# Scores of two chunked recurrences: one native float32 product, or three passes of split operands

## The chip, the cores and the metric

The kernel runs on one core of a Trainium2 chip. The metric is device time in microseconds (us) of one execution. A run executes the whole block once, from the inputs in device memory to the output in device memory.

## The reference, cut to what matters

The block has one layer over 1024 positions of width 1024. It normalises `x`, multiplies by one wide input matrix, and feeds three branches: an mLSTM (matrix memory with gates), a differential attention and a retention. Their outputs are merged, projected, and followed by a gated feed-forward layer. The mLSTM and the retention are recurrences over chunks, with 4 heads of width 256 each. What the change touches is the score product in both of them:

```
# mLSTM, per chunk
s = einsum('blhd,bshd->bhls', qj, kj) * w_intra
num = einsum('bhls,bshe->blhe', s, vj) + einsum('blhd,bhde->blhe', qj, C) * w_int_t
C_new = w_old * C + einsum('bhs,bshd,bshe->bhde', w_k, kj, vj)
# retention, per chunk
s = einsum('blhd,bshd->bhls', qj, kj) * dmask
o = einsum('bhls,bshe->blhe', s, vj) + einsum('blhd,bhde->blhe', qj, R) * xi
R_new = chunk_decay * R + einsum('hs,bshd,bshe->bhde', zeta, kj, vj)
```

All inputs and outputs are float32.

## The kernel before

**Split operands.** Nearly all products are made of three passes. A float32 operand is split by `split_sbuf` (L104 to L106) into a high part, which ScalarE casts to the type float32r (L105), and a low part, the rest, which VectorE subtracts (L106). `mm3` (L108 to L113) then sums three matmuls into one bank of PSUM: high by high (L111), high by low (L112), low by high (L113). The first two have the same stationary operand. A native float32 matmul, without a split, is used in a few places; the scores of the recurrences are one (L690).

**The recurrences.** Both are run in chunks of 128 positions, 8 chunks in each of 4 heads, so 32 chunks each and 64 in all. `pipelined` (L777) goes through the chunks. For each it loads the next chunk's tile `ch` from device memory (`chunk_of`, L639; 128 partitions, eight blocks of 128 columns: two of queries, two of keys, two of a gate, two of values), and then calls three parts. `start` makes the scores (`scores_t`, L687), turns keys and values round by transposes on TensorE (`natural_k`, `natural_v`, L645 to L668), multiplies the scores by the mask (L733 in the mLSTM, L946 in the retention) and splits what the next part multiplies (L739, L950). `end` of the chunk before turns its result round and stores it (L693 to L701). `middle` multiplies scores by values and queries by the carried state into one bank (`chunk_products`, L676), and updates the state (L764, L968) and splits it (`split_state`, L703).

**The queries for the state.** In the mLSTM the queries are scaled per position (L735) and stand in one tile `w` beside the masked scores, 384 columns in all, which are split together. In the retention they are not scaled, but they are copied beside the scores all the same (L948), and split with them (L950). The first chunk of a head has no state and splits 128 columns only.

**The order of work.** Between the three parts of a chunk, `weave` (L1470) takes steps of dense work, 2.6 per unit of weight that `pipelined` yields: two units a chunk. A dense step is here one of seven products of a block of the input projection (`follow`, L373), 12 passes of 512 columns each, with its evacuation and the split of a later weight. A scheduler then writes out the order of each engine's queue from priorities (the order of the program) and from its own estimate of what will be ready; an instruction that it holds to be late is passed by ready ones. On the chip each queue runs in the order written.

**Buffers.** Tiles of up to 512 float32 columns come from one group of 14 buffers (`half_tile`, L96). Score tiles in PSUM come from a group of four banks, those of the dense work from another group of four.

Of the kernel before, what the change touches and what calls it, by code (L numbers as in the profile page):

```python
# [9 lines left out]
F32R = mybir.dt.float32r  # L10
# [5 lines left out]
P = 128  # L16
# [24 lines left out]
def trunk(ctx: ExitStack, tc: tile.TileContext, x, norm_gains, w_in, mlstm_conv, mlstm_gate_bias,  # L41
          diff_lambda, diff_subln, w_mlstm_out, w_diff_out, w_ret_out, w_out, w_ffn_in, w_ffn_out,
          c_ident, c_dist, c_tri, c_ret, c_retcol, c_reset, out):
    nc = tc.nc
# [21 lines left out]
    def psum(dense=False):  # L66

        return psp.tile([P, HALF], F32, tag="d" if dense else "m", bufs=N_D if dense else 8 - N_D, name=nm("ps"))
# [27 lines left out]
    def half_tile(shape=(P, HALF), dtype=F32):  # L96
        return pool.tile(list(shape), dtype, tag="s2k", bufs=N_H, name=nm("s2k"))
# [6 lines left out]
    def split_sbuf(hi, lo, src):  # L104
        nc.scalar.copy(hi, src)  # L105
        nc.vector.tensor_sub(lo, src, hi.bitcast(F32))  # L106

    def mm3(ps, lhs, rhs, start, stop, more=False):  # L108

        (lh, ll), (rh, rl) = lhs, rhs  # L110
        nc.tensor.matmul(ps, lh, rh, start=start, stop=False, skip_group_check=more)  # L111
        nc.tensor.matmul(ps, lh, rl, start=False, stop=False, skip_group_check=more)  # L112
        nc.tensor.matmul(ps, ll, rh, start=False, stop=stop, skip_group_check=more)  # L113
# [556 lines left out]
    def both(t):  # L670
        return t[:, 0], t[:, 1]

    def cols_at(t, a, b):
        return t[0][:, a:b], t[1][:, a:b]

    def chunk_products(u, d, n):  # L676

        num = psum()
        v = both(u["v"])
        mm3(num[:, :n], cols_at(u["w"], 0, P), v, True, u["c"] == 0)  # L680
        if u["c"] > 0:
            for j in range(2):
                st = tuple(t[:, j, :] for t in d["parts"])
                mm3(num[:, :n], cols_at(u["w"], P + j * P, 2 * P + j * P), st, False, j == 1)
        return num

    def scores_t(ch):  # L687
        ps = psum()
        for j in range(2):
            nc.tensor.matmul(ps[:, :P], ch[:, 2 + j, :], ch[:, j, :], start=j == 0, stop=j == 1)  # L690
        return ps[:, :P]

    def finish_chunk(u, spill):  # L693

# [15 lines left out]
    def mlstm_core():  # L710
        def start(u):
            hd, c = u["hd"], u["c"]
            d = ml[hd]
            ch = u["ch"]
            if c == 0:
                wt = d["wt"] = big([P, NT, P], name="wt")
                nc.sync.dma_start(wt, rows_dram[0, hd:hd + 1, :].rearrange("o (c l) -> o c l", l=P).broadcast_to([P, NT, P]))
                wib = d["wib"] = big([P, S], name="wib")
                nc.sync.dma_start(wib, rows_dram[1, hd:hd + 1, :].broadcast_to([P, S]))

                wk = d["wk"] = small([P, NT], "wk")
                nc.vector.tensor_tensor(wk, wt[:, :, P - 1], u_col[:, :, hd], op=ALU.add)
                nc.scalar.activation(wk, wk, AF.Exp)
                nc.vector.tensor_tensor(wt, wt, tri.unsqueeze(1).broadcast_to([P, NT, P]), op=ALU.add)
                for i in range(NT):
                    nc.scalar.activation(wt[:, i, :], wt[:, i, :], AF.Exp, bias=u_col[:, i, hd:hd + 1])
            s_ps = scores_t(ch)
            if c < NT - 1:
                u["kw"] = natural_k(ch, d["wk"][:, c:c + 1])
            u["v"] = natural_v(ch, True)  # L730
            n = 3 * P if c > 0 else P
            w = half_tile([P, n])
            nc.vector.scalar_tensor_tensor(w[:, :P], s_ps, HD ** -0.5, d["wt"][:, c, :], op0=ALU.mult, op1=ALU.mult)  # L733
            if c > 0:
                nc.vector.scalar_tensor_tensor(w[:, P:].rearrange("p (j l) -> p j l", j=2), ch[:, 0:2, :], HD ** -0.5,  # L735
                                               d["wib"][:, c * P:(c + 1) * P].unsqueeze(1).broadcast_to([P, 2, P]),
                                               op0=ALU.mult, op1=ALU.mult)
            u["w"] = half_tile([P, n], F32R), half_tile([P, n], F32R)
            split_sbuf(*u["w"], w)  # L739

        def middle(u):
            hd, c = u["hd"], u["c"]
            d = ml[hd]
            num = chunk_products(u, d, VA)


            ss = square_sum(num[:, :HD], HD, "m")
            den = small([P, 1], "den", bufs=4)
            nc.vector.tensor_scalar(den, num[:, HD:HD + 1], -1.0, em_col[:, c, hd:hd + 1], op0=ALU.mult, op1=ALU.max)
            nc.vector.tensor_tensor(den, num[:, HD:HD + 1], den, op=ALU.max)  # L750
            nc.gpsimd.tensor_scalar(den, den, den, EPS, op0=ALU.mult, op1=ALU.mult)
            fac = small([P, 1], "fac", bufs=4)
            factor(fac, ss, 1.0 / HD, den)
            if c < NT - 1:
                if c == 0:
                    d["st"] = small([P, 2, VA], "st", bufs=1)
                for j in range(2):
                    kv = psum()
                    mm3(kv[:, :VA], cols_at(both(u["kw"]), j * P, (j + 1) * P), both(u["v"]), True, True)
                    st = d["st"][:, j, :]  # L760
                    if c == 0:
                        nc.vector.tensor_copy(st, kv[:, :VA])
                    else:
                        nc.vector.scalar_tensor_tensor(st, st, d["wib"][:, c * P + P - 1:c * P + P], kv[:, :VA],  # L764
                                                       op0=ALU.mult, op1=ALU.add)
                split_state(d)
            u["hn"] = small([P, HD], "hk", bufs=2)
            nc.scalar.activation(u["hn"], num[:, :HD], AF.Copy, scale=fac)

        def end(u):  # L770
            finish_chunk(u, b_dram[0])
            if u["c"] == NT - 1:
                ml[u["hd"]].clear()

        yield from pipelined(m_dram, 0, start, middle, end)
# [152 lines left out]
    def ret_core():  # L928
        retm = half_tile([P, MH, P])
        nc.scalar.dma_start(retm, c_ret)  # L930

        over = small([P, MH], "over", bufs=1)
        nc.vector.reciprocal(over, retc[:, 2 * MH:3 * MH])
        nc.vector.tensor_scalar(over, over, EPS / HD, None, op0=ALU.mult)

        def start(u):
            hd, c = u["hd"], u["c"]
            d = rt[hd]
            ch = u["ch"]
            s_ps = scores_t(ch)  # L940
            if c < NT - 1:
                u["kw"] = natural_k(ch, retc[:, hd:hd + 1])
            u["v"] = natural_v(ch, False)
            n = 3 * P if c > 0 else P
            w = half_tile([P, n])
            nc.vector.tensor_mul(w[:, :P], s_ps, retm[:, hd, :])  # L946
            if c > 0:
                nc.vector.tensor_copy(w[:, P:].rearrange("p (j l) -> p j l", j=2), ch[:, 0:2, :])  # L948
            u["w"] = half_tile([P, n], F32R), half_tile([P, n], F32R)
            split_sbuf(*u["w"], w)  # L950

        def middle(u):
            hd, c = u["hd"], u["c"]
            d = rt[hd]
            num = chunk_products(u, d, HD)
            ss = square_sum(num[:, :HD], HD, "r")
            fac = small([P, 1], "rfac", bufs=4)
            factor(fac, ss, 1.0 / HD, over[:, hd:hd + 1])
            if c < NT - 1:
                kv = psum()  # L960
                for j in range(2):
                    mm3(kv[:, j * HD:(j + 1) * HD], cols_at(both(u["kw"]), j * P, (j + 1) * P), both(u["v"]), True, True)
                kv = kv.rearrange("p (j e) -> p j e", j=2)
                if c == 0:
                    d["st"] = small([P, 2, HD], "st", bufs=1)
                    nc.vector.tensor_copy(d["st"], kv)
                else:
                    nc.vector.scalar_tensor_tensor(d["st"], d["st"], (1.0 - 2.0 ** (-5.0 - hd)) ** P, kv, op0=ALU.mult, op1=ALU.add)  # L968
                split_state(d)
            u["hn"] = small([P, HD], "hk", bufs=2)  # L970
            nc.scalar.activation(u["hn"], num[:, :HD], AF.Copy, scale=fac)

        def end(u):
            finish_chunk(u, b_dram[2])
            if u["c"] == NT - 1:
                rt[u["hd"]].clear()

        yield from pipelined(r_dram, 4 * MH, start, middle, end)


# [387 lines left out]
    for b in BRANCHES:  # L1368
        for o in range(0, KT, 2):
            c = C_G + b * D + o * P  # L1370
# [76 lines left out]
    ps = psum()  # L1447
# [92 lines left out]
```

## Time and profile before

| what | value |
|---|---|
| median of 3 runs | 2629.19 us (2627.92 to 2631.38) |
| the profiled execution, its own time | 2628.78 us |
| its span, first to last instruction | 2627.0 us |
| TensorE (PE) busy | 2520.3 us, 96% |
| VectorE (DVE) busy | 1650.2 us, 63% |
| ScalarE (ACT) busy | 1245.9 us, 47% |
| GpSimd (POOL) busy | 331.8 us, 13% |

PE is the multiplying array, PEld the loading of its stationary operand, which has a record of its own for each matmul. A matmul's record lasts longer than the step to the next one, since matmuls are pipelined: what a matmul costs a full array is the time from its start to the next start. In the timelines, `L690` and the like are lines of the kernel; `s2k` are the tiles of `half_tile`; `x4` says that four like instructions were merged into one row. A native float32 matmul shows two PE records.

### The profile page before, as it was taken

Reading aid. Unit: us, or ns where it says so; the run is one execution under the profiler, and the core shown is the slowest. Engines: PE = TensorE matmul, PEld = TensorE weight load, DVE = VectorE, ACT = ScalarE, POOL = GpSimd, SP = SyncE. Lnnn points to the kernel's source line nnn. Section 1 sums busy time; section 2 is a strip of 40 time slices with the busy share of each in tenths; the row PEclk is TensorE's granted clock in tenths of the full one; section 3 lists DMA queues with packets and bytes.
Section 4 is the critical chain, followed back from the end, with each engine's and each line's share of the span. In section 5 each row is a group of like instructions: output and inputs, shape, how many; then the busy total and the mean of one; then the engine's idle time right before and its main releaser. Section 6 shows DMA issues by size and latency. Waiting matters only on the chain.

```text
span 2627.0 us, 35171 instructions
## 1 busy us (share of the span) xinstructions
PE 2520.3 (96%) x12061; PEld 2058.6 (78%) x12061; DVE 1650.2 (63%) x3164; ACT 1245.9 (47%) x2562; POOL 331.8 (13%) x657
## 2 busy tenths in 40 slices
PE   6989999999999999999999988999989999999997
PEld 5868887888888888888878776778877888888885
DVE  7767777666656666555556665653468655656756
ACT  6554554444444444444446555542365333334444
POOL 0001111000000000000003223332121110110000
PEclk9999999999999999999999999999999999999999
DMA  4344345454445545444467566745443333327342
GB/s 127 95 125 137 115 132 153 136 150 123 127 139 161 169 145 150 137 134 121 138 193 178 140 184 157 189 157 188 144 137 112 101 104 97 105 97 288 113 143 78
DMA packets 402078, 368.93 MB, mean 140 GB/s; under 512 B 18957, under 2 KB 302046, under 8 KB 401898
## 3 DMA queue, kind: packets, MB, share of 16 engines
q1 hardware_dynamic: 399424, 364.45, 46.3%
q10 hardware_dynamic: 2474, 2.22, 0.3%
q8 instruction: 95, 1.56, 0.3%
q14 instruction: 85, 0.70, 0.1%
HBM read 249.92 MB, written 116.69 MB: 140 GB/s over the span
## 4 chain that ended last, share of the span: by engine, by line
PE 73%; issue 12%; DVE 5%; ACT 4%; POOL 3%; DMA 3%; SPq 1%; ACTq 0%; DVEq 0%; POOLq 0%
PE ps L112 22%; PE ps L113 22%; PE ps L111 22%; PE ps L874 2%; PE ps L837 1%; DMA s2k<-branch 1%; ACT sb L844 1%; POOL dfac L221 1%; PE ps L690 1%; PE ps L649 1%; POOL fv L220 1%; DVE sb L839 1%; POOL xr L208 1%; DMA ws<-in_w_in_dram 1%; DVE wl L106 0%
## 5 line engine op out<-in xcount | busy, mean ns | idle before, releaser
L105 ACT CAST wh<-ws 128x512 fp32r<-128x512 f32 (+1 forms) x622 | 385.1, 623 | 708.5 <-PE ps L112 514.1
L106 DVE TENSOR_TENSOR wl<-ws,wh 128x512 fp32r<-128x512 f32 (+1 forms) x622 | 449.8, 726 | 255.7 <-ACT wh L105 245.5
L315 DVE TENSOR_TENSOR ws<-ws,ws 128x512 f32<-128x512 f32 x234 | 160.8, 689 | 105.7 <-DMA ws<-in_w_in_dram 60.5
L111 PE MATMUL ps<-bh,wh 128*128 128x512 f32 x384 | 155.5, 405 | 1.6 <-ACT bh L105 1.6
L112 PE MATMUL ps<-bl,wh 128*128 128x512 f32 x384 | 152.5, 397 | 0.2 <-DVE bl L106 0.2
L113 PE MATMUL ps<-bh,wl 128*128 128x512 f32 x384 | 152.1, 396 | 0.0
L328 ACT COPY s2k<-ps 128x512 f32<-128x512 f32 x234 | 135.8, 581 | 11.2 <-PE ps L113 11.0
L111 PE MATMUL ps<-S2h,wh 128*128 128x512 f32 x312 | 125.7, 404 | 4.9 <-ACT s2k L328 4.9
L111 PE MATMUL ps<-A11h,wh 128*128 128x512 f32 x312 | 126.3, 405 | 2.7 <-ACT A11h L272 2.7
L112 PE MATMUL ps<-S1l,wh 128*128 128x512 f32 x312 | 123.5, 396 | 2.7 <-DVE S1l L106 2.7
L111 PE MATMUL ps<-S3h,wh 128*128 128x512 f32 x312 | 125.2, 401 | 0.9 <-ACT s2k L328 0.9
L111 PE MATMUL ps<-S1h,wh 128*128 128x512 f32 x312 | 124.2, 401 | 1.8 <-ACT S1h L105 1.7
L111 PE MATMUL ps<-A22h,wh 128*128 128x512 f32 x312 | 124.9, 400 | 0.8 <-DVE s2k L454 0.6
L112 PE MATMUL ps<-wl,wh 128*128 128x512 f32 x308 | 120.5, 392 | 4.8 <-DVE wl L106 4.8
L111 PE MATMUL ps<-S4h,wh 128*128 128x512 f32 x312 | 124.8, 400 | 0.0
L111 PE MATMUL ps<-A12h,wh 128*128 128x512 f32 x312 | 124.7, 400 | 0.0
L112 PE MATMUL ps<-S2l,wh 128*128 128x512 f32 x312 | 124.5, 400 | 0.0
L112 PE MATMUL ps<-A11l,wh 128*128 128x512 f32 x312 | 124.3, 398 | 0.1
L112 PE MATMUL ps<-A12l,wh 128*128 128x512 f32 x312 | 123.8, 397 | 0.5 <-DVE A12l L280 0.5
L113 PE MATMUL ps<-S2h,wl 128*128 128x512 f32 x312 | 124.1, 398 | 0.0
L113 PE MATMUL ps<-A11h,wl 128*128 128x512 f32 x312 | 124.0, 398 | 0.0
L113 PE MATMUL ps<-A12h,wl 128*128 128x512 f32 x312 | 123.9, 397 | 0.0
(301 smaller groups left out, 6434.1 us busy)
## 6 DMA issues: line engine op xcount, KB each, us to landing
ws<-in_w_in_dram SPq DMA_DIRECT2D x112, 512.0 KB, 4.5
ws<-in_w_ffn_in_dram SPq DMA_DIRECT2D x44, 512.0 KB, 4.3
m_dram<-s2k SPq DMA_DIRECT2D x64, 256.0 KB, 2.0
ch<-m_dram SPq DMA_DIRECT2D x32, 512.0 KB, 5.3
r_dram<-s2k SPq DMA_DIRECT2D x64, 256.0 KB, 2.3
ch<-r_dram SPq DMA_DIRECT2D x32, 512.0 KB, 4.7
qk_dram<-s2k SPq DMA_DIRECT2D x64, 256.0 KB, 2.7
dk<-qk_dram SPq DMA_DIRECT2D x64, 256.0 KB, 5.6
```

The source lines that it names most:

```text
L105: nc.scalar.copy(hi, src)
L106: nc.vector.tensor_sub(lo, src, hi.bitcast(F32))
L111: nc.tensor.matmul(ps, lh, rh, start=start, stop=False, skip_group_check=more)
L112: nc.tensor.matmul(ps, lh, rl, start=False, stop=False, skip_group_check=more)
L113: nc.tensor.matmul(ps, ll, rh, start=False, stop=stop, skip_group_check=more)
L208: nc.gpsimd.tensor_tensor(dst, t, expo[:, 0:1], op=ALU.pow)
L220: nc.gpsimd.tensor_scalar(t, ss, scale, extra, op0=ALU.mult, op1=ALU.add)
L221: nc.gpsimd.tensor_tensor(dst, t, expo[:, 0:1], op=ALU.pow)
L315: nc.vector.tensor_sub(*sub[r])
L328: nc.scalar.copy(t, ps)
L649: nc.tensor.transpose(ps[:, j * P:(j + 1) * P], ch[:, i + j, :], ident)
L874: nc.tensor.matmul(o_ps[:, :P], u["at"][kb // 4][:, half_cols(kb)], v[:, kb, :], start=kb == 0, stop=kb == qb)
```

## The change

`scores_t` is given two new tiles of 512 columns, splits the chunk's queries and keys into them (one cast on ScalarE, one subtraction on VectorE), and makes the scores with `mm3`, two times three passes, in place of two native float32 matmuls. The mLSTM drops the parts after the scores. The retention keeps them: `chunk_products` takes its queries from them (`u["q"]`), so the copy of L948 goes, and only the 128 columns of the scores are split, into one tile of two parts.

```
     def chunk_products(u, d, n):
...
-                mm3(num[:, :n], cols_at(u["w"], P + j * P, 2 * P + j * P), st, False, j == 1)
+                q = at_block(u["q"], j) if "q" in u else cols_at(u["w"], P + j * P, 2 * P + j * P)
+                mm3(num[:, :n], q, st, False, j == 1)
         return num
 
-    def scores_t(ch):
+    def scores_t(ch, parts):
         ps = psum()
+        split_sbuf(*parts, ch[:, 0:4, :])
         for j in range(2):
-            nc.tensor.matmul(ps[:, :P], ch[:, 2 + j, :], ch[:, j, :], start=j == 0, stop=j == 1)
+            mm3(ps[:, :P], at_block(parts, 2 + j), at_block(parts, j), j == 0, j == 1)
         return ps[:, :P]
+
+    def at_block(t, i):
+        return t[0][:, i, :], t[1][:, i, :]
...  # mLSTM, start
-            s_ps = scores_t(ch)
+            parts = half_tile([P, 4, P], F32R), half_tile([P, 4, P], F32R)
+            s_ps = scores_t(ch, parts)
...  # retention, start
-            s_ps = scores_t(ch)
+            parts = half_tile([P, 4, P], F32R), half_tile([P, 4, P], F32R)
+            s_ps = scores_t(ch, parts)
...
-            n = 3 * P if c > 0 else P
-            w = half_tile([P, n])
-            nc.vector.tensor_mul(w[:, :P], s_ps, retm[:, hd, :])
-            if c > 0:
-                nc.vector.tensor_copy(w[:, P:].rearrange("p (j l) -> p j l", j=2), ch[:, 0:2, :])
-            u["w"] = half_tile([P, n], F32R), half_tile([P, n], F32R)
+            w, two = half_tile([P, P]), half_tile([P, 2, P], F32R)
+            nc.vector.tensor_mul(w, s_ps, retm[:, hd, :])
+            u["w"] = both(two)
             split_sbuf(*u["w"], w)
+            u["q"] = parts
```

## Rows read from the trace of the kernel before

**Rows 1.** The page: TensorE's busy time, and the chain that ended last, by engine.
```profile
PE 2520.3 (96%) x12061; PEld 2058.6 (78%) x12061; DVE 1650.2 (63%) x3164; ACT 1245.9 (47%) x2562; POOL 331.8 (13%) x657
...
PE 73%; issue 12%; DVE 5%; ACT 4%; POOL 3%; DMA 3%; SPq 1%; ACTq 0%; DVEq 0%; POOLq 0%
```

**Rows 2.** Stretches, busy us: mLSTM chunks, retention chunks, attention; PE, PEld, DVE, ACT, POOL, clock.
```profile
148.00:716.00 568.00, 561.66 (x2754) 464.18 (x2755) 391.41 (x766) 274.70 (x566) 57.65 (x210) 1.00 0.45 133
717.00:1308.00 591.00, 589.06 (x2934) 486.73 (x2933) 354.70 (x637) 281.78 (x571) 30.11 (x67) 1.00 0.50 144
1345.00:1745.00 400.00, 360.20 (x2010) 297.29 (x2009) 243.72 (x763) 224.62 (x633) 120.97 (x264) 0.98 0.63 168
```

**Rows 3.** Waits of PE from 148 to 1308 us: total us, times, longest.
```profile
PE ps L690 <- DMA ch<-m_dram: 4.2, 2, 3.6
PE ps L111 <- ACT s2k L328: 1.5, 2, 1.3
PE ps L113 <- DVE s2k L106: 1.1, 2, 0.6
...
PE ps L111 <- ACT s2k L105: 0.9, 1, 0.9
```

**Rows 4.** The instructions of line 690, all 64 chunks: ns minimum, median, maximum.
```profile
L690 PE MATMUL ps<-ch x256: 270/275/348, 148.2 to 1289.2; 128*128 128x128 f32 x128
```

**Rows 5.** Timeline of PE around one chunk's scores: start us, us, then the instruction.
```profile
347.29 0.40 PE L112 MATMUL ps<-A11l,wh 128*128 128x512 f32 x1
347.53 0.39 PE L113 MATMUL ps<-A11h,wl 128*128 128x512 f32 x1
347.76 0.60 PE L690 MATMUL ps<-ch 128*128 128x128 f32 x4
348.20 0.60 PE L649 MATMUL ps<-ident,ch 128*128 128x128 f32 x4
348.56 0.48 PE L113 MATMUL ps<-A12h,wl 128*128 128x512 f32 x1
348.87 0.40 PE L111 MATMUL ps<-A12h,wh 128*128 128x512 f32 x1
```

**Rows 6.** Timeline of PE in the attention: four float32r passes of 128 columns.
```profile
1398.00 0.49 PE L864 MATMUL ps<-ident,s2k 128*128 128x128 f32 x3
1398.24 0.64 PE L837 MATMUL ps<-dk,dq 128*128 128x128 f32 x4
1398.72 0.29 PE L890 MATMUL ps<-ident,hk 128*128 128x128 f32 x1
```

**Rows 7.** Timeline of PEld in the same stretch: the loads of those four passes.
```profile
1398.22 0.53 PEld L837 LDWEIGHTS ps<-dk,dq 128*128 128x128 f32 x4
1398.69 0.14 PEld L890 LDWEIGHTS ps<-ident,hk 128*128 128x128 f32 x1
```

**Rows 8.** Timeline of PE: first of 15 passes of 256 columns, and what follows them.
```profile
844.26 0.28 PE L111 MATMUL ps<-s2k,s2k 128*128 128x256 f32 x1
...
846.01 0.39 PE L111 MATMUL ps<-S1h,wh 128*128 128x512 f32 x1
```

**Rows 9.** Groups from 717 to 1308 us: busy us, mean ns, idle before and releasers.
```profile
L106 DVE TENSOR_TENSOR wl<-ws,wh 128x512 fp32r<-128x512 f32 x177 | 121.3, 685 | 67.6 <-ACT wh L105 64.0 <-PE ps L690 3.4
L105 ACT CAST wh<-ws 128x512 fp32r<-128x512 f32 x176 | 109.2, 620 | 195.0 <-PE ps L112 162.6 <-issue 28.1 <-DVE ws L315 1.6
...
L106 DVE TENSOR_TENSOR s2k<-s2k,s2k 128x384 fp32r<-128x384 f32 x29 | 16.2, 557 | 10.0 <-ACT s2k L105 9.9
L105 ACT CAST s2k<-s2k 128x384 fp32r<-128x384 f32 x29 | 14.9, 513 | 25.7 <-DVE s2k L948 24.4 <-DVE s2k L733 1.1
...
L948 DVE COPY s2k<-ch 128x256 f32<-128x256 f32 x28 | 7.9, 282 | 0.0
L105 ACT CAST s2k<-s2k 128x128 fp32r<-128x128 f32 x4 | 1.2, 308 | 2.3 <-DVE s2k L946 2.3
L106 DVE TENSOR_TENSOR s2k<-s2k,s2k 128x128 fp32r<-128x128 f32 x4 | 1.1, 286 | 0.7 <-ACT s2k L105 0.7
```

## The prediction, made before the change was built

> **What bounds the kernel now.** I read the page first: TensorE is busy 96% of the span and holds 73% of the chain that ended last; VectorE and ScalarE are at 63% and 47% [rows 1]. Since a share over the span can hide stages with other limits, I then asked for the stretches in which the change lies. In the mLSTM chunks PE is busy 561.66 of 568 us, in the retention chunks 589.06 of 591, at a granted clock of 1.00, the upper level, 2.4 GHz; VectorE has 177 and 236 us free there, ScalarE 293 and 309 [rows 2]. So both stretches are TensorE's: a PE step saved or added there is saved or added in full, and work on VectorE or ScalarE is free as long as it does not make PE wait. PE's idle time in both stretches is 6.3 + 1.9 = 8.3 us, which is all that any better order there could still win. The attention that follows has 40 us of it [rows 2], but its program is not touched.
>
> The third view, the list of waits, says what little PE waits for: the largest entry is the load of a chunk, 4.2 us in two waits. What the change adds more of, an operand that is split on ScalarE and VectorE just before PE multiplies it, costs PE 1.1 us (two waits for the low part) and 0.9 us (one for the high part) now [rows 3]. There are 64 such splits of masked scores and 56 of states in the 64 chunks, so 2.0 us over 120 edges.
>
> **The change part by part.** *Scores removed.* Line 690 has 256 PE records [rows 4]: 64 chunks with two native float32 matmuls, each recorded twice. Their four records start at 347.76 and what follows starts at 348.20, so they cost 0.44 us a chunk, 0.11 us a record [rows 5]. The durations (275 ns) overlap and are not the cost. The pass of 512 columns ahead of them takes 347.76 - 347.53 = 0.23 us, as any other there, so nothing is lost in going over to native float32.
>
> *Scores added.* Six float32r passes of 128 columns a chunk. The trace has no run of six, but the attention has four in a row: they start at 1398.24 and the next instruction at 1398.72, 0.48 us for four, 0.12 us each [rows 6]. Four times the columns take 0.23 us [rows 5], and twice the columns take (846.01 - 844.26)/15 = 0.117 us [rows 8]. So the cost does not go down from 256 to 128 columns, and the loads show why: every pass has a load of its own (the page counts 12061 of both, so also the two passes of `mm3` that share their stationary operand load it twice [rows 1]), and the four loads of the short passes stand 1398.69 - 1398.22 = 0.47 us apart in all, 0.117 us each [rows 7]. A short pass lasts as long as the next load. Upper end: 6 x 0.12 = 0.72 us, 0.28 us more than now. Lower end of the columns alone, half of a 256-column pass each: 6 x 0.058 = 0.35 us, 0.09 us less than now. I take the rows nearest to the case, the 0.117 us of the loads, for five passes, and the columns' 0.058 us for one, because the second load can be made while the 512-column pass ahead still runs: 5 x 0.117 + 0.058 = 0.64 us. That is 0.20 us more a chunk than 0.44, and 64 x 0.20 = 12.8 us on an engine without room.
>
> The Trainium skill has a rule against this. "FP8 and Floating Point Precision", section "TensorE Precision Notes", says that true float32 takes four passes through the array and reduced float32 one. By it three passes would be three quarters of the price, an estimate that makes the kernel faster. The trace agrees with the four (two records of 0.11 us for 128 columns) but not with the three quarters.
>
> *The split of queries and keys.* One cast and one subtraction of 512 columns a chunk: 0.620 us on ScalarE and 0.685 us on VectorE, from the same form on weights [rows 9]. Over 64 chunks 39.7 us and 43.8 us. In the retention 28 chunks now split 128 columns in place of 384, 0.308 for 0.513 us and 0.286 for 0.557 us, and lose the copy of 0.282 us [rows 9]: 5.7 us less on ScalarE, 15.5 us less on VectorE. What stays, 34 us and 28 us, is covered by the 602 and 413 us that these engines have free in both stretches. If that cover were gone, the price would show in a late evacuation of a dense product.
>
> *The new wait.* The scores now wait for cast and subtraction; before, they needed only the chunk's load, which is issued a chunk ahead. On PE's queue the transposes of keys and values (L649) and the next dense products stand behind the scores. Best case: the scheduler writes ready dense passes ahead of the scores, as it does for the masked scores now, and each of the 64 edges costs what the 120 do, 2.0/120 us: 1.1 us. Worst case: each time PE stands still for 0.62 + 0.69 = 1.3 us, 84 us in all. The nearest row is the first, since it is the same helper on the same engines, so I take 1.1 us. Below zero it can't be, as nothing that PE waits for gets earlier by more than PE's 8.3 us of idle time. Behind the split on ScalarE and VectorE stand the evacuations of dense products; each comes at most 0.7 us later, and the four banks of the dense work hold more than one product of 2.8 us (12 passes of 0.23).
>
> *The shorter chain in the retention.* Masked scores go without the copy and with a shorter split, about 0.28 + 0.2 + 0.27 = 0.75 us sooner to the products. PE idles 1.9 us in that whole stretch [rows 2]: cost and gain 0. The products with the state keep their passes and sizes: 0.
>
> *Buffers.* Two more tiles a chunk from the group of 14; in the retention two parts live on to the products, where one pair of 384 columns lived before and one tile does now. No engine wait for a store that frees one is among PE's rows [rows 3]. Taken as 0; the upper end is in the second rival. No transfer is added or moved on any queue.
>
> *Sum.* The profiled execution took 2628.8 us (span 2627.0 and 1.8 around it): 2628.8 + 12.8 + 1.1 = 2642.7. It lies 0.4 us below the median of the runs, so 2643 is what I forecast. With passes between 0.17 us and 0.28 us dearer and a few us for an order written anew, this case spans 2637 to 2652.
>
> **The rivals.** *Passes are paid by their columns* (the other side). If the loads of float32r can be made ahead, because the six passes are mixed with passes of 512 columns or because loads are pulled forward, each costs 0.058 us: 64 x (0.35 - 0.44) = -5.8 us, 2623. It decides where a short pass stands behind a long one. For it: one such step per chunk is likely, and the rule on passes named above. Against: the four in a row cost 0.12 us [rows 6], and all six become ready at the same moment.
>
> *The split comes late.* The scheduler's estimate of ScalarE and VectorE is too good, and PE stands for part of the 1.3 us in most chunks, or the two tiles make an evacuation wait for a buffer. For a quarter to a half of the worst case, 21 to 42 us on top: 2664 to 2685. For it: ScalarE's casts of weights already wait for PE to release their buffer (162.6 us in the retention [rows 9]), and a cast that waits holds the split behind it. Against: the splits that exist cost PE 2.0 us.
>
> *The shared stationary operand is loaded once.* Then a chunk has four loads as before, and 0.47 us [rows 7] stands for 0.44: +2 us, 2631, no change that can be told. Against: equal counts of loads and matmuls [rows 1]. The Trainium skill, "TensorE: Matmul & The Clock Gate", section "Back-to-back issue gap", gives some 81 ns for a sustained load and matmul of 128 columns; by that estimate six passes are 0.49 us, and the time would come out in this case too. The trace shows 0.117 to 0.12 us, and the trace decides.
>
> **How the numbers follow.** Forecast 0.72, late split 0.13, passes by columns 0.07, no change 0.08. Differences within 0.2% (5.3 us) can't be told from none. The likeliest case lies wholly above 2634.4; the late split too. So faster 0.07, same 0.08, slower 0.85. The range takes in the likeliest case, from 2634, where the edge of no change begins, up to the lower part of the late split: 2634 to 2664.
>
> **What would show it.** After the change the scores should be 384 PE records, from their start to the transposes 0.6 to 0.7 us, with loads 0.11 to 0.12 us apart. PE's busy time in the stretch from 148 us to the end of the retention should rise by 11 to 15 us, and the stretch be longer by that; ScalarE about 34 us busier, VectorE about 28 us. The waits of PE for a split should stay at a few us. The forecast is wrong if the scores are spread singly among long passes, if PE's waits for L105 or L106 grow to tens of us, or if the attention, which is not touched, moves by more than the term.

## The result, and the profile after

The changed kernel takes 2676.44 us (median of 4 runs, 2670.93 to 2682.96), the kernel before 2629.01 us: 1.0185 times as long, 95% interval 1.0173 to 1.0198. That is 47 us slower, where 14 were forecast and 2664 us was the upper end of the range. The direction was right, and the case that came is the second rival, the late split. The profiled execution took 2674.37 us, its span 2672.6.

The page of the changed kernel, the two lines that answer [rows 1]. TensorE is still the bound, busy for 95% of the span. The shares of the chain can't be set beside those of before: they add up to 74%, since the chain could be followed back only to 698.51 us, and of that part TensorE holds 57 of 74, about 77%.

```profile
PE 2546.9 (95%) x12189; PEld 2064.0 (77%) x12189; DVE 1673.8 (63%) x3200; ACT 1277.0 (48%) x2626; POOL 334.9 (13%) x657
...
PE 57%; DVE 4%; issue 4%; ACT 4%; POOL 3%; DMA 2%; SPq 0%; DVEq 0%; POOLq 0%; ACTq 0%
```

128 more matmuls, 31 us more on ScalarE and 24 us more on VectorE, where 34 and 28 were reckoned: the added work is about what was foreseen. The same three stretches as in [rows 2], moved to where they now lie (length; busy us of PE, PEld, DVE, ACT, POOL; clock):

```profile
148.00:747.00 599.00, 576.40 (x2819) 467.49 (x2818) 413.28 (x803) 294.01 (x600) 58.99 (x210) 1.00 0.43 127
748.00:1357.00 609.00, 602.59 (x2994) 491.07 (x2993) 360.54 (x634) 294.07 (x601) 30.63 (x67) 1.00 0.48 138
1394.00:1794.00 400.00, 361.08 (x2015) 298.02 (x2014) 244.36 (x763) 225.34 (x635) 122.36 (x266) 0.98 0.62 169
```

The mLSTM chunks are 31 us longer, the retention chunks 18, and the attention is as it was. PE's idle time in the two is 22.6 + 6.4 = 29.0 us in place of 8.3. The clock did not change. The waits of PE in both stretches, which answer [rows 3], and after them those of the loads on PEld (us in total, times, longest):

```profile
PE ps L111 <- ACT s2k L105: 13.0, 16, 1.7
PE ps L112 <- DVE s2k L106: 11.0, 16, 1.5
PE ps L111 <- ACT s2k L328: 4.3, 4, 2.2
```

```profile
PEld ps L111 <- ACT s2k L105: 27.0, 40, 2.2
PEld ps L112 <- DVE s2k L106: 24.5, 56, 1.9
```

The waits for a split, which cost PE 2.0 us before, cost it 24.0 us now. The loads tell it more plainly, because a load's record (0.19 us) is shorter than a pass's and hides less of the wait behind it: in the two stretches, 40 loads of the kind of the first score pass waited for a cast of the split, and 56 of the kind of the second for a subtraction. PE's own record hides a part of each wait, since a pass counts as busy for 0.28 to 0.4 us and the next could start after 0.06 to 0.23 us.

What [rows 5] showed of one chunk before is, in a good chunk after:

```profile
706.85 0.40 PE L113 MATMUL ps<-A12h,wl 128*128 128x512 f32 x1
707.08 0.23 PE L111 MATMUL ps<-s2k 128*128 128x128 f32 x1
707.14 0.28 PE L112 MATMUL ps<-s2k,s2k 128*128 128x128 f32 x1
707.25 0.27 PE L113 MATMUL ps<-s2k,s2k 128*128 128x128 f32 x1
707.36 0.28 PE L111 MATMUL ps<-s2k 128*128 128x128 f32 x1
707.47 0.28 PE L112 MATMUL ps<-s2k,s2k 128*128 128x128 f32 x1
707.59 0.28 PE L113 MATMUL ps<-s2k,s2k 128*128 128x128 f32 x1
707.70 0.62 PE L649 MATMUL ps<-ident,ch 128*128 128x128 f32 x4
```

Six passes from 707.08 to 707.70, 0.62 us; the first steps on after 0.06 us, the others after 0.11. The forecast had 0.64, made up in the same way (five passes by their loads and one by its columns). And in a bad chunk, PE and then VectorE:

```profile
810.01 0.33 PE L111 MATMUL ps<-s2k 128*128 128x128 f32 x1
810.17 0.62 PE L649 MATMUL ps<-ident,ch 128*128 128x128 f32 x4
812.15 0.33 PE L112 MATMUL ps<-s2k,s2k 128*128 128x128 f32 x1 [1.36 <-DVE s2k L106]
812.32 0.28 PE L113 MATMUL ps<-s2k,s2k 128*128 128x128 f32 x1
```

```profile
810.20 0.69 DVE L315 TENSOR_TENSOR ws<-ws,ws 128x512 f32<-128x512 f32 x1 [1.94 <-DMA ws<-in_w_in_dram]
810.81 0.69 DVE L106 TENSOR_TENSOR wl<-ws,wh 128x512 fp32r<-128x512 f32 x1
811.41 0.68 DVE L106 TENSOR_TENSOR s2k<-ch,s2k 128x512 fp32r<-128x512 f32 x1
```

The first pass needs only the high parts and runs at 810.01; the second needs the low parts. Their subtraction stands on VectorE's queue behind two instructions for a dense weight, and the first of those waits for a transfer until 810.20. So the subtraction starts at 811.41, and PE, once it has done the transposes (L649), stands still until 812.15, with dense passes written behind the scores. This is the rule and not the exception: at the median of the 64 chunks the subtraction ends 0.7 us after the first score pass has started. Only in 10 of the 64 do the six passes stand together, with nothing between them. Summed from PE's timeline over all chunks, from when each score pass could have started to the start of what follows, the scores take 81.9 us in place of 34.5: 47.4 more, and the span grew by 45.6.

### The profile page after: what moved, and what is told of

Read it like the earlier page. It is cut to its first block, busy times and chain, and to the rows that moved or that the text cites. A ratio compares the mean times of both kernels' runs of the same rounds, so it can differ in the third digit from the quotient of the medians.

```text
span 2672.6 us, 35588 instructions
## 1 busy us (share of the span) xinstructions
PE 2546.9 (95%) x12189; PEld 2064.0 (77%) x12189; DVE 1673.8 (63%) x3200; ACT 1277.0 (48%) x2626; POOL 334.9 (13%) x657
## 4 chain that ended last, share of the span: by engine, by line
PE 57%; DVE 4%; issue 4%; ACT 4%; POOL 3%; DMA 2%; SPq 0%; DVEq 0%; POOLq 0%; ACTq 0%
PE ps L112 18%; PE ps L113 17%; PE ps L111 17%; PE ps L881 2%; PE ps L844 1%; ACT sb L851 1%; POOL dfac L221 1%; DMA s2k<-branch 1%; DVE wl L106 1%; DVE sb L846 1%; POOL fv L220 1%; PE ps L871 0%; ACT junk L214 0%; POOL xr L208 0%; PE ps L649 0%
## 5 line engine op out<-in xcount | busy, mean ns | idle before, releaser
L105 ACT CAST wh<-ws 128x512 fp32r<-128x512 f32 (+1 forms) x622 | 385.4, 623 | 696.8 <-PE ps L112 510.2
L106 DVE TENSOR_TENSOR wl<-ws,wh 128x512 fp32r<-128x512 f32 (+1 forms) x622 | 446.5, 721 | 254.3 <-ACT wh L105 249.0
L328 ACT COPY s2k<-ps 128x512 f32<-128x512 f32 x234 | 135.7, 581 | 11.7 <-PE ps L113 11.6
L112 PE MATMUL ps<-s2k,s2k 128*128 128x256 f32 (+2 forms) x416 | 119.4, 287 | 11.3 <-DVE s2k L106 11.0
```

Of the source, the lines that this page charges most:

```text
L328: nc.scalar.copy(t, ps)
```

## The experiments

The theory was: some 12 us are the short passes, the rest is PE waiting for a split that stands behind other work in ScalarE's and VectorE's queues. The rivals: the extra load on these engines or the two extra buffers delay the dense products; or the short passes are dearer in place than in a row. Each ratio is to the kernel before, run beside it on the same chip. It took 2627.41 us beside the first four runs (splits, wait, passes, early split), 2627.95 us beside the next four (copy by ScalarE, copy by VectorE, split on GpSimd, wide queries), and 2625.71 us beside the last four; differences in us are to these.

**Splits without their use.** In the changed kernel:

```
-            mm3(ps[:, :P], at_block(parts, 2 + j), at_block(parts, j), j == 0, j == 1)
+            nc.tensor.matmul(ps[:, :P], ch[:, 2 + j, :], ch[:, j, :], start=j == 0, stop=j == 1)
```

> The changed kernel, but the scores are native float32 products of the chunk's tile again; the split of queries and keys (cast, subtraction, both tiles) stays, and the retention still takes its queries from it. So the ScalarE and VectorE work and the buffers of the change are there, the wait of the scores and the six short passes are not. Theory (the change's 47 us are about 34 of waiting for the split and 12 of short passes): 2627 to 2634 us, no change that can be told. Rival A (the extra work on ScalarE and VectorE, or the two tiles out of 14, delay the dense products): 2650 to 2670. Rival B (short passes alone): also about 2629, told apart by the next two.

Measured 2627.89 us, 1.0002 (0.9992 to 1.0013). The added work on ScalarE and VectorE and the two tiles of the 14 cost nothing; rival A falls. In the mLSTM nothing reads the two tiles here, so they come free sooner than in the change; the early split below, in which they live longer, covers that.

**The wait without the passes.** In the kernel before:

```
     def scores_t(ch):
         ps = psum()
+        t = half_tile([P, 4, P]), half_tile([P, 4, P])
+        nc.scalar.copy(t[0], ch[:, 0:4, :])
+        nc.vector.tensor_tensor(t[1], ch[:, 0:4, :], t[0], op=ALU.max)
...
-            nc.tensor.matmul(ps[:, :P], ch[:, 2 + j, :], ch[:, j, :], start=j == 0, stop=j == 1)
+            nc.tensor.matmul(ps[:, :P], t[j][:, 2 + j, :], t[j][:, j, :], start=j == 0, stop=j == 1)
```

> The kernel before, with the wait of the change but not its passes: the scores stay two native float32 products, but the first reads a copy of queries and keys made by ScalarE, and the second one made by VectorE from the chunk's tile and that copy (a maximum of both, 512 columns). The values are those of before. Theory: the wait alone brings about 34 us: 2655 to 2672 us. Rival B (short passes alone): 2629 to 2634.

Measured 2654.17 us, 1.0110 (1.0094 to 1.0125): 26.8 us, 0.8 us below the expected range. The waits of PE in both stretches (L690 is the copy by ScalarE, L691 the one by VectorE, L693 the scores):

```profile
PE ps L693 <- ACT s2k L690: 15.3, 16, 2.9
PE ps L111 <- ACT s2k L328: 8.1, 6, 2.6
PE ps L693 <- DVE s2k L691: 3.6, 6, 1.1
```

The scores' wait is there, and the scores have no float32r pass at all. So is a second one, for the evacuation of a dense product, its copy out of PSUM (L328): 8.1 us where it was 1.5 [rows 3].

**The passes without the wait.** In the kernel before:

```
-        t = u["ch"] = big([P, 8, P], name="ch")
+        t = u["chr"] = big([P, 8, P], F32R, "ch")
+        u["ch"] = t[:, :, :].bitcast(F32)
...
-            nc.tensor.matmul(ps[:, :P], ch[:, 2 + j, :], ch[:, j, :], start=j == 0, stop=j == 1)
+            mm3(ps[:, :P], (r[:, 2 + j, :],) * 2, (r[:, j, :],) * 2, j == 0, j == 1)
```

> The kernel before, with the passes of the change but not its wait: the chunk's tile is loaded as float32r and the scores are six float32r passes straight from it, with no split. The low parts are left out, and the product of the high parts is summed three times, so the scores are not those of the reference; times alone count. Theory: six passes at 0.61 to 0.67 us for 0.44, times 64: plus 11 to 15 us, 2640 to 2645 us. Rival B (short passes are dearer in their place, each switch costing array time): 2665 to 2680. Rival C (paid by columns): 2621 to 2626.

Measured 2640.64 us, 1.0052 (1.0035 to 1.0069): 13.2 us, as expected; rivals B and C fall. The short passes alone, 13.2 us, and the wait alone, 26.8, make 40 of the 47 us. The 7 left over were not isolated. The sums from PE's timeline say where they lie: in the retention the scores cost 20.2 us more than before in the changed kernel, but 6.3 in the wait alone and 5.6 in the passes alone; in the mLSTM it is 27.3 against 17.3 and 5.8.

**The split half a chunk earlier.** In the changed kernel:

```
-        split_sbuf(*parts, ch[:, 0:4, :])
...
+    def split_early(u):
+        u["parts"] = half_tile([P, 4, P], F32R), half_tile([P, 4, P], F32R)
+        split_sbuf(*u["parts"], u["ch"][:, 0:4, :])
...  # pipelined, after end(before)
+            if n + 1 < len(units):
+                split_early(units[n + 1])
             yield 0.5
             middle(u)
```

> The changed kernel with the split of queries and keys moved ahead: it is issued in the middle of the chunk before, after that chunk's predecessor is stored, so cast and subtraction are done when the scores come up. Same work and same passes; the two tiles live half a chunk longer. Theory: the waits of PE for L105 and L106 go back to a few us and the time to that of the passes alone, 2638 to 2648 us. Rival A (load or buffers): 2665 to 2690, for two tiles living longer can only make it worse.

Measured 2640.91 us, 1.0058 (1.0043 to 1.0073). The same passes, casts, subtractions and tiles, and 13.5 us above the kernel before in place of 47: 34 us less. PE's waits (the first rows, both stretches):

```profile
PE ps L111 <- ACT s2k L328: 5.8, 5, 2.6
PE ps L111 <- ACT s2k L105: 3.1, 5, 1.1
PE ps L111 <- DVE s2k L483: 1.6, 1, 1.6
PE ps L112 <- DVE s2k L106: 0.8, 1, 0.8
```

The waits for the split (second and fourth row) are 3.1 + 0.8 us in place of 24.0. The subtraction now ends before the first score pass starts, 7.2 us before it at the median in the retention and 1.5 us in the mLSTM; in the changed kernel it ends 0.7 us after that start. This settles the cause: the place of the split in the order, not its work. The time that is left equals that of the passes alone.

**Which queue.** The kernel before, with native scores that read a copy by one engine alone:

```
+        t = half_tile([P, 4, P])
+        nc.scalar.copy(t, ch[:, 0:4, :])                                   # one run
+        nc.vector.tensor_tensor(t, ch[:, 0:4, :], ch[:, 0:4, :], op=ALU.max)  # the other
```

> The kernel before, with native float32 scores that read a copy of queries and keys made by ScalarE alone. Theory, more closely: ScalarE's queue is the late one, because its casts of weights wait for TensorE to release their buffers and it evacuates the dense product that has just ended; of the 27 us of the wait alone 15 to 25 come from here: 2643 to 2653 us. If the two queues count alike: 2640 to 2643.

> The kernel before, with native float32 scores that read a copy of queries and keys made by VectorE alone (a maximum of the tile with itself, 512 columns). Theory: VectorE's queue alone is late by less, 3 to 12 us: 2631 to 2640 us. If VectorE's queue is the late one: 2645 to 2655, and the run with ScalarE alone near 2629.

Measured 2645.57 us, 1.0067 (1.0050 to 1.0084), with ScalarE and 2644.91 us, 1.0067 (1.0052 to 1.0082), with VectorE. The run with ScalarE lies in its expected range, the one with VectorE 5 us above its own. So the closer theory, that ScalarE's queue is the late one, was wrong: they count alike, 17 to 18 us each. They do so in different places. PE's waits, with ScalarE in the mLSTM and in the retention:

```profile
PE ps L692 <- ACT s2k L690: 12.8, 14, 2.5
...
PE ps L692 <- ACT s2k L690: 2.4, 2, 1.9
```

and with VectorE:

```profile
PE ps L692 <- DVE s2k L690: 9.1, 11, 2.8
...
PE ps L692 <- DVE s2k L690: 6.6, 8, 1.2
```

**The split on a third engine.** In the changed kernel, and in the one with the early split:

```
-        split_sbuf(*parts, ch[:, 0:4, :])
+        nc.gpsimd.tensor_copy(parts[0], ch[:, 0:4, :])
+        nc.gpsimd.tensor_tensor(parts[1], ch[:, 0:4, :], parts[0].bitcast(F32), op=ALU.subtract)
```

> The changed kernel, with both halves of the split on GpSimd, whose queue holds little else and no evacuation of a dense product. Theory (the split is late because it stands in ScalarE's and VectorE's queues behind other work): a chunk's tile lands well before it is used, so the split is ready in time, and only the short passes are left: 2638 to 2648 us. If the split is late for another reason (the chunk's tile lands late, or cast and subtraction themselves are too long), 2665 to 2690 as the changed kernel, or more, as GpSimd takes longer for them.

> The changed kernel with the split of queries and keys on GpSimd and issued half a chunk ahead, as in the early split. With the split on GpSimd alone the retention's scores were on time and the mLSTM's were not: there the split stood behind the normalising factor of the chunk before, whose input comes late. Theory (the place in an in-order queue decides, whatever the engine): the early place mends it, only the short passes are left, 2638 to 2646 us. If GpSimd is too slow for the mLSTM, or the tile of the chunk lands too late: 2655 to 2675.

Measured 2671.36 us, 1.0168 (1.0153 to 1.0183), and with the early place 2661.10 us, 1.0138 (1.0123 to 1.0153). Both times the theory missed, and the time lies in the range that was given for the case that the chunk's tile lands late or GpSimd is too slow. Of the first, the waits of PE in the mLSTM (first two rows) and in the retention (the last):

```profile
PE ps L112 <- POOL s2k L692: 15.5, 19, 1.2
PE ps L111 <- POOL s2k L691: 8.3, 11, 1.7
...
PE ps L112 <- POOL s2k L692: 1.4, 3, 0.6
```

In the retention it does what was expected: the scores cost 8.5 us more than before, where they cost 20.2 in the changed kernel and 5.6 with the passes alone. The split stands at the same place of the program there, but in a queue that holds little else, and PE hardly waits. That is the best evidence that other work in ScalarE's and VectorE's queues makes the split late. The mLSTM spoils the time. The second run shows why. PE's waits for the split in it, all in the mLSTM, and its groups on GpSimd (busy us, mean ns, idle before and releasers):

```profile
PE ps L112 <- POOL s2k L698: 5.8, 7, 1.1
...
PE ps L111 <- POOL s2k L697: 4.2, 5, 1.1
```

```profile
L698 POOL TENSOR_TENSOR s2k<-ch,s2k 128x512 fp32r<-128x512 f32 x64 | 92.1, 1439 | 82.3 <-issue 23.1 <-DVE s2k L106 16.0 <-PE ps L512 9.0
L697 POOL CAST s2k<-ch 128x512 fp32r<-128x512 f32 x64 | 44.3, 693 | 431.3 <-DMA ch<-m_dram 233.2 <-PE ps L113 34.0 <-DVE s2k L106 28.8
```

GpSimd's cast waits for the chunk's tile itself, 233 us, all of it from the mLSTM's tensor. The wait of an engine with little to do costs nothing by itself, but it shows that the split can't start earlier there. In the kernel before, the load of the mLSTM chunk of [rows 5] was issued at 338.77 us and its scores began at 347.76; with the 5.1 us that such a load takes to land, 4 us are left. The load of a retention chunk whose scores began at 848.80 was issued at 807.91, 36 us of room. These two are typical: from issue to scores it is 9.0 us at the median of the mLSTM's 32 chunks and 42.1 us in the retention's. (First row: mLSTM. Second: retention.)

```profile
338.77 0.52 SPq L643 DMA_DIRECT2D ch<-m_dram  x1
...
807.91 0.52 SPq L643 DMA_DIRECT2D ch<-r_dram  x1
```

So in most chunks of the mLSTM the split has no more than some 4 us. A cast and a subtraction of 0.6 and 0.7 us fit in if nothing stands ahead of them; GpSimd's 0.69 + 1.44 us behind the normalising factor of the chunk before do not. In 10 of the 32 chunks of the second run's mLSTM the subtraction ends after the first score pass has started. That last step is read from the trace; an earlier load was not tried.

The waits for the split and the 13 us of the passes do not make up the 35 us by which the second run is slower. A part of the rest is TensorE's clock. After PE has stood still for the split, the granted clock in this stretch is 0.51, the lower level, 1.2 GHz, and passes of 512 columns then stand 0.43 us apart in place of 0.23 (the stretch as in [rows 2], then PE):

```profile
207.60:211.00 3.40, 3.40 (x12) 2.73 (x11) 3.40 (x9) 1.00 (x2) 0.00 (x0) 0.51 0.22 64
```

```profile
206.94 0.33 PE L112 MATMUL ps<-s2k,s2k 128*128 128x128 f32 x1 [0.83 <-POOL s2k L698]
...
208.86 0.63 PE L111 MATMUL ps<-S2h,wh 128*128 128x512 f32 x1
209.28 0.63 PE L112 MATMUL ps<-S2l,wh 128*128 128x512 f32 x1
```

The six steps from 208.43 to 210.98 us take 2.55 us in place of 1.40. The clock falls like this five times in the recurrences of this run, four times in those of the first, and never in those of the changed kernel. At 1.2 us each that is some 6 us, an estimate from this one place.

**One recurrence alone.** In the changed kernel, the mLSTM's call goes back to native scores (`scores_n` is `scores_t` as it was before):

```
-            parts = half_tile([P, 4, P], F32R), half_tile([P, 4, P], F32R)
-            s_ps = scores_t(ch, parts)
+            s_ps = scores_n(ch)
```

> The change in the retention alone; the mLSTM has native float32 scores and no split of queries and keys. From the trace of the changed kernel, where the scores cost TensorE 20 us more in the retention and 27 in the mLSTM: 2643 to 2652 us. If one stretch's late split makes the other's worse, less: 2636 to 2643.

Measured 2645.43 us, 1.0086 (1.0064 to 1.0107): 19.7 us, within the first range, and near the 18 us by which the retention's stretch is longer in the trace of the changed kernel; the mLSTM alone was not run.

**The queries alone.** In the changed kernel, native scores in both; in the retention:

```
+            parts = half_tile([P, 2, P], F32R), half_tile([P, 2, P], F32R)
+            s_ps = scores_n(ch)
...
+            if c > 0:
+                split_sbuf(*parts, ch[:, 0:2, :])
             u["q"] = parts
```

> The other part of the change alone: native float32 scores in both recurrences; in the retention the queries for the state are split straight from the chunk's tile, without the copy, and the scores are split by themselves. VectorE and ScalarE lose about 8 and 0 us against the kernel before, TensorE nothing: 2625 to 2632 us, no change that can be told.

Measured 2624.92 us, 0.9997 (0.9987 to 1.0006): no change. What the change takes off VectorE in the retention buys nothing.

**Fewer loads.** From the early split, high and low queries side by side in one tile, and high and low keys in another, so that the split is two casts and two subtractions of 256 columns:

```
-            mm3(ps[:, :P], at_block(parts, 2 + j), at_block(parts, j), j == 0, j == 1)
+            q, k = parts
+            nc.tensor.matmul(ps[:, :2 * P]..., k[:, j, 0, :], q[:, j, :, :], start=j == 0, stop=False, ...)
+            nc.tensor.matmul(ps[:, :P], k[:, j, 1, :], q[:, j, 0, :], start=False, stop=j == 1, ...)
+        t = half_tile([P, P])
+        nc.vector.tensor_copy(t, ps[:, P:2 * P])
+        nc.vector.tensor_add(t, ps[:, :P], t)
```

> The changed kernel with the early split, and high and low queries side by side: the high keys are multiplied with both in one pass of 256 columns, the low keys with the high queries in one of 128, so four passes and four loads a chunk in place of six; VectorE adds the two halves (a copy and an addition of 128 columns). The sum is the same three products. If a short pass costs its load (0.11 to 0.12 us whatever the columns up to 256): 0.46 us a chunk for 0.44, 2627 to 2634 us, no change to the kernel before. If a pass is paid by its columns, nothing is gained over the early split: 2638 to 2646.

> The four passes with high and low queries side by side, with the split on GpSimd, half a chunk ahead. In the run of the wide queries the scores cost TensorE less than before (0.41 us a chunk for 0.44), but waits for ScalarE's evacuations of dense products cost it some 10 us. Theory: these come from the casts and subtractions added to ScalarE's and VectorE's queues, and go with them: 2624 to 2632 us, like the kernel before or a little faster. If they come from the new order of the queues in itself: 2635 to 2642, as in that run.

Measured 2638.09 us, 1.0041 (1.0026 to 1.0056); with the split on GpSimd 2657.69 us, 1.0118 (1.0103 to 1.0133). The theory missed both times, and the second time lies above both ranges that were given. The first lies at the lower edge of the range for passes that are paid by their columns, but by luck, for the passes did as the load rule has it:

```profile
845.82 0.29 PE L693 MATMUL ps<-s2k,s2k 128*128 128x256 f32 x1
845.95 0.23 PE L694 MATMUL ps<-s2k,s2k 128*128 128x128 f32 x1
846.01 0.33 PE L693 MATMUL ps<-s2k,s2k 128*128 128x256 f32 x1
846.18 0.22 PE L694 MATMUL ps<-s2k,s2k 128*128 128x128 f32 x1
846.24 0.62 PE L649 MATMUL ps<-ident,ch 128*128 128x128 f32 x4
```

Four passes, the three products of the change, take 0.42 us where six took 0.62 and native float32 0.44. The 10 us above the kernel before stand elsewhere, and all of them in the mLSTM: from the scores of its second chunk to those of its last the first run takes 542.0 us, the kernel before 529.9, while in the retention it is 525.5 against 527.8. There the four passes are no dearer than native float32. In the first of the two, PE's waits begin with these:

```profile
PE ps L111 <- ACT s2k L328: 7.4, 10, 2.6
PE ps L693 <- DVE s2k L106: 3.6, 6, 1.0
```

L328 is the evacuation of a dense product, 1.5 us before [rows 3]. The second run was to tell whether the casts on ScalarE's queue or the new order cause it; the mLSTM's late split on GpSimd (11.2 us of PE's waits) covers the answer, so that stays open. A third possibility was not tried by itself: in both runs VectorE has a copy and an addition more in each chunk, 0.28 and 0.29 us. No version tried beats the kernel before.

## Why the prediction was wrong

- **The bound** was right: both stretches are TensorE's, and what PE lost there is the result (47.4 us of PE's time against 45.6 us of span). Its busy share is a poor measure of that loss: it was to rise by 11 to 15 us in the two stretches and rose by 28.3, since a part of the waiting is hidden in the records.
- **The short passes** were right in size: 12.8 us forecast, 13.2 measured by themselves, and 0.62 us for six in the trace against 0.64. The loads of float32r set the pace, as [rows 7] had it. Neither estimate from the Trainium skill came true: six passes take 0.62 us, which is not three quarters of 0.44, and not 0.49 either. "FP8 and Floating Point Precision", section "TensorE Precision Notes", in the Trainium skill gives four passes for true float32. The trace agrees with that: a native product of 128 columns takes 0.22 us, and half a float32r pass of 256 columns 0.058 us. Of reduced float32 the section says that it is cut to the engine's own precision; that this makes one pass is the prediction's reading. "TensorE: Matmul & The Clock Gate", section "Back-to-back issue gap", in the Trainium skill gives 81 ns for a load and matmul of 128 columns. Here it is 0.11 us. With four passes, which have as many loads as native float32, the price is 0.42 us for 0.44.
- **The load on ScalarE and VectorE, the buffers, and the copy that went** were right: nothing, nothing and nothing, each shown by a run.
- **The new wait** is the step that failed. It was put at 1.1 us, from the splits that exist: "the same helper on the same engines". With the passes' 13 us taken off, it cost some 34, of which the wait alone shows 26.8. The row was real, but its neighbour was not like it. The split masked scores are multiplied in `middle`, a weight of 1.5 after `start`, so nearly four dense products of 2.8 us lie between the split and its use; the split state is used a whole chunk later. The new split is used by the next instruction in the program. The early split gives it such a distance, as far as the load allows, and PE's waits for a split go from 24.0 us to 3.9. In proportion, the worst case in the text, 84 us, was a better guide than "the nearest row": 34 is 40% of 84, and thirty times 1.1. The sign that was named for this, waits of tens of us for L105 or L106, came.
- **"Before, they needed only the chunk's load, which is issued a chunk ahead"** was true of the program's order and not of the chip in the mLSTM: 4 us from landing to use against 36 in the retention, in the chunks shown. [Rows 3] had the hint, two waits for `ch<-m_dram` and none for the retention's.
- **The range** stopped at 2664, the lower end of the second rival, which was given 0.13. Its price, 21 to 42 us on top, held (34); its reason was half right, since VectorE's queue is as late as ScalarE's.

## What to carry to other kernels

The price of a new wait does not follow from who makes the operand but from how much ready work lies between the maker and the user in each queue: look for an existing edge with the same distance, not the same helper. If there is none, take the full latency of the makers, once per use, as the upper end (here the wait came to 40% of it), look at what stands ahead in the makers' queues, and move the maker ahead before anything else. Passes over few columns (128 here) are paid by the loads of their stationary operand, so count loads, and put what shares a stationary operand side by side in the moving one.

## What was not expected of the hardware

- A pass of 128 columns steps on after 0.06 us if a longer pass runs ahead of it, and after 0.11 us in a row of its kind; after a pass of 256 columns 0.06 us as well. The three products of both halves, made as four matmuls, thus take 0.42 us a chunk, less than native float32's 0.44.
- GpSimd takes 1.33 us in the first of its two runs and 1.44 us in the second for a subtraction of 128x512 that takes VectorE 0.69 us; its cast of the same size takes 0.67 to 0.69 us, near ScalarE's 0.62.
